# Three single buffers become two or three, and memory attention is handed out in three parts behind the projections

## The chip, the core and the metric

The kernel runs on one core of a Trainium2 chip. The core has five engines that each take their instructions in order: TensorE (PE in the profile), VectorE (DVE), ScalarE (ACT), GpSimd (POOL) and the sync engine (SP), which in this kernel issues every DMA. The metric is device time in microseconds for one execution of the whole program. Before the change it is 2147.47 us, the median of three runs (2147.37 to 2157.03).

## The reference, cut to what matters

One layer over 4096 rows of width 1024. A normalized input is projected once, and three groups of heads read the projection; their gated outputs go through one output projection.

```python
h = _rms(x, norm_gain)
proj = h @ w_in                          # u, v, gate | q, k, v, gate | mem q, mem gate
y_g = _chunked_gmlp(g_u, g_v, ...) * silu(g_gate)      # 4 heads, mixes 128 rows of a chunk
q, k = _rms(a_q, ...), _rms(a_k, ...)                  # 8 heads of 64
y_a = _dilated_attention(q, k, v) * silu(a_gate)       # windows (128,1) (512,4) (2048,16)
qn = _rms(m_q, ...)                                    # 4 heads into 256 memory rows
p = softmax(qn @ mk.T / sqrt(64))
y_m = (p @ mv) * silu(m_gate)
x = x + concat(y_g, y_a, y_m) @ w_out
```

The dilated attention runs the same head at three dilations and weights them by their softmax denominators. The inputs have wide gains, so a true row maximum is taken before each exponential, and every product is made of two halves in 16 bits (a high and a low part) to keep the accuracy.

## The kernel before, in words

The rows are cut into 32 tiles of 128. There are four stretches of the span. Pass A (to about 423 us) normalizes and transposes the rows and projects v and half of q and k. Pass B (`pass_b`, about 423 to 948 us) projects the other half and the attention gate. Pass C (`pass_c`, about 948 to 1774 us) does the gating group and the memory attention, tile by tile; in an iteration n it projects tile n with `wC1` (tile `pc1`), and tile n-2 (`LAG`) with `wC2` and `wC3` (`pc2`, `pc3`). The last stretch merges all and multiplies with `w_out` (`fps`).

The dilated attention runs beside passes B and C as a second stream, `side`, which `merge` advances by so many steps per step of the main one, at a higher priority. For each of the 8 heads it has a part that finds row maxima (`attn_max`) and a main part (`attn_main`); the maxima of head h+1 are found during the main part of head h. In `attn_max`, PE multiplies `qn` and `kp` into `pa` (line 489), DVE takes maxima into `mx` (line 496), these become `mv`, PE transposes them (`pm`, line 513), ACT copies them into a tile of rows `rw` (line 514), a DMA spreads the row out into `cm` (line 515), and DMAs put the result into row 64 of `q2` (line 534), without which the second product of `s` (line 588) can't start. The tiles `qn` and `kp` have one buffer each, so the next head's load (lines 335 to 337) begins after the last `pa` of this head. In `attn_main`, ACT copies the finished outputs from PSUM into `ot` (line 618), from which DMAs store them (lines 623 and 627).

Memory attention of a tile (`mem_attn`) makes a high part `qd` (ACT, line 794) and a low part `q2t` (DVE, line 795), transposes `qd` by a DMA, multiplies it with the memory keys into `mpa` (line 804), takes maxima, puts them into column 64 of `q2t` (line 807), and transposes `q2t` by a DMA into `qm` (line 808); then come scores `ms`, the exponential, `mo`, and `ym`.

The order on each engine is not the order of the code: a scheduler places instructions by their priority (mostly their place in the code, with the offset for the second stream) and by the times that it foresees. A small edit can therefore move rows far away. An engine stands at its next row until that can go, and everything behind waits too; for SP that holds for every DMA of the kernel. Four buffers bear on the change: `rw` has one, of the two dilations 1 and 4 that use it in turn; `ot` has two; `q2t` one for all tiles; and PSUM tiles have two of each tag.

Of the kernel before, what the change touches and what calls it, by code (L numbers as in the profile page):

```python
# [2 lines left out]

# [6 lines left out]
F16 = mybir.dt.float16  # L10
# [8 lines left out]
P = 128  # L19
T = 4096  # L20
D = 1024
NT = T // P
KT = D // P
# [48 lines left out]
def tile_hybrid_layer(ctx, tc, x, mem, norm_gain, w_in, gv_gain, wsT, gb, aqg, akg,  # L72
                      mem_gain, w_kv, mqg, mkg, w_out, out):
    nc = tc.nc
    V, S, G, TE, Q = nc.vector, nc.scalar, nc.gpsimd, nc.tensor, nc.sync
# [6 lines left out]
    def ps_tile(tag, shape, dt, name):  # L82
        return pp.tile(shape, dt, tag="po" if tag == "tr" else tag, name=name)
# [135 lines left out]
    def proj(ps, xt, w, n, c=0):  # L219
        for k in range(KT):  # L220
            for a, b in ((0, 0), (0, 1), (1, 0)):
                TE.matmul(ps[:, :n], xt[:, a, k, :], w[:, b, k, c:c + n],  # L222
                          start=(k == 0 and a == 0 and b == 0), stop=(k == KT - 1 and a == 1))


    def load_rows(pool, src, nm):
# [63 lines left out]
    pm = ctx.enter_context(tc.tile_pool(name="pm", bufs=2))  # L290
# [33 lines left out]
    K1m = cp.tile([P, 4, 256], F16, name="K1m")  # L324
    K2m = cp.tile([65, 4, 256], F16, name="K2m")
# [23 lines left out]
    with tc.tile_pool(name="pA", bufs=2) as pA:  # L349
# [33 lines left out]
        for i in range(2):  # L383
            for n in range(NL):
                if i == 0:
                    vts[n] = pA.tile([P, NH, VW], F16, name=f"vt{n}", tag="vt", bufs=5)
                ps = ps_tile("pj", [P, 512], F32, f"pv{n}_{i}")
# [8 lines left out]
        for n in range(NT):  # L396
# [37 lines left out]
            if n >= NL:  # L434
                ps = ps_tile("pj", [P, 512], F32, f"pv{n}")
# [4 lines left out]
            ps = ps_tile("pj", [P, 512], F32, f"pq{n}")  # L440
# [13 lines left out]
            if n == 12:  # L454
                wM, scM = got("wM")
                for j in range(2):
                    mT = mTs[:, j]
                    ps = ps_tile("pj", [P, 512], F32, f"pm{j}")
# [19 lines left out]
    def attn_max(h, qn, kp):  # L478
        mx = at.tile([P, 96], F32, name=f"mx{h}", tag="mx", bufs=1)
        for ci, d in enumerate(DILS):  # L480
            nb = NT // d
            for u in range(16):
                pa = ps_tile("pa", [P, 2, 256], F32, f"pa{h}_{ci}_{u}")
                for i in range(2):
                    bi = 2 * u + i
                    r, b = bi // nb, bi % nb
                    q0 = r + b * P * d
                    w = 256 if b else 128
                    TE.matmul(pa[:, i, 256 - w:256], qn[:, q0:q0 + (P - 1) * d + 1:d],  # L489
                              packed(kp, d, r, max(b - 1, 0), w), start=True, stop=True)  # L490
                for i in range(2):
                    bi = 2 * u + i
                    w = 256 if bi % nb else 128
                    mc = 64 + (bi % 2) * 16 + bi // 2 if d == 16 else ci * 32 + bi
                    jk = at.tile([P, 256], BF16, name=f"jk{h}_{ci}_{bi}", tag="jk", bufs=1)
                    V.tensor_tensor_reduce(jk[:, :w], pa[:, i, 256 - w:256],  # L496
                                           masks[d][:, 256 - w:256],
                                           1.0, -3e38, ALU.add, ALU.max,
                                           mx[:, mc:mc + 1])
                yield  # L500
        mv = at.tile([P, 96], F16, name=f"mv{h}", tag="mv", bufs=1)
        V.tensor_scalar(mv, mx, -(2.0 ** -15), asg[:, 3:4], ALU.mult, ALU.add)
        cm = at.tile([32, 4, P], F16, name=f"cm{h}", tag="cm", bufs=1)
        Q.dma_start(m_d[h].rearrange("(b p r) -> p b r", b=2, r=16),
                    mv[:, 64:96].rearrange("p (b r) -> p b r", b=2))
        Q.dma_start(cm[:, 2, :], m_d[h].rearrange("(n p) -> n p", p=P))
        for ci, d in enumerate(DILS[0:2]):
            nb = NT // d
            rw = at.tile([nb, P * d], F16, name=f"rw{h}_{ci}", tag="rw", bufs=1)
            pt = ps_tile("tr", [P, 4, P], F16, f"pm{h}_{ci}")  # L510
            for r in range(d):
                c0 = ci * 32 + r * nb
                TE.transpose(pt[:nb, r, :], mv[:, c0:c0 + nb], idh)
            S.copy(rw.rearrange("b (p r) -> b r p", r=d), pt[:nb, :d, :])
            Q.dma_start(cm[:, ci, :], rw.rearrange("b (n p) -> b n p", p=P))
        yield
        V.tensor_tensor(cm[:, 0, :], cm[:, 0, :], cm[:, 1, :], ALU.min)
        ca, cb = (cm[:, i, :].rearrange("n (j r) -> n j r", r=R16) for i in (0, 2))
        V.tensor_tensor(cm[:, 3, :].rearrange("n (r j) -> n j r", r=R16), ca, cb, ALU.min)
        cms[h] = cm  # L520
        yield
# [24 lines left out]
    def attn_main(h, q1, k1):  # L546
# [6 lines left out]
        for ci, d in list(enumerate(DILS))[::ORD]:  # L553
# [20 lines left out]
            for r in range(d):  # L574
                prev = None
                for b0 in range(0, nb, 2):
# [19 lines left out]
                    def pv(r=r, b0=b0, ph=ph, pl=pl, prev=prev, ci=ci, d=d, nb=nb, vblk=vblk, og=og):  # L596
                        for i in range(2):
# [16 lines left out]
                                          start=False, stop=(j == len(terms) - 1))  # L614
                            if slot == 3:
                                ot = at.tile([P, 4, 65], F32, name=f"ot{h}_{ci}_{r}_{b}", tag="ot",
                                             bufs=2)
                                S.copy(ot, o)
                                if d == 4:
                                    ov = o_d[ci].rearrange("(b m r j) h c -> r b m j h c", b=nb,  # L620
                                                           r=d, j=8)
                                    for i in range(4):
                                        Q.dma_start(ov[r, b - 3 + i, :, :, h, :], ot[:, i, :])
                                else:
                                    ov = o_d[ci].rearrange("(x p) h c -> p x h c", p=P)
                                    x1 = r * nb + b + 1
                                    Q.dma_start(ov[:, x1 - 4:x1, h, :], ot)
# [155 lines left out]
    wC1, scC1 = got("wC1")  # L783
    wC3, scC3 = got("wC3")
    fz = cp.tile([P, 4], F32, name="fz")
    q2ts = [pm.tile([P, 4, P], F16, name=f"q2t{i}", bufs=1) for i in range(1)]
    V.memset(q2ts[0], 0.0)

    qms = [None]

    def mem_attn(n, qn):
        qd = pm.tile([P, 4, 2, HD], F16, name=f"qd{n}", tag="hl", bufs=2)
        q2t = q2ts[0]
        S.copy(qd, qn.unsqueeze(2).broadcast_to([P, 4, 2, HD]))
        V.tensor_sub(q2t[:, :, 0:64], qn, qd[:, :, 0, :])
        if n % 2 == 0:
            qms[0] = pm.tile([P, 2, 2, 4, P], F16, name=f"qm{n}", tag="stg", bufs=2)
        Q1m, Q2m = qms[0][:, n % 2, 0], qms[0][:, n % 2, 1]
        Q.dma_start_transpose(Q1m, qd.rearrange("p s a c -> p (s a c)"))
        m4 = pm.tile([P, 4], F32, name=f"m4{n}", tag="m4")  # L800
        for hp in range(2):
            pa = ps_tile("pa", [P, 2, 256], F32, f"mpa{n}_{hp}")
            for i in range(2):
                TE.matmul(pa[:, i, :], Q1m[:, 2 * hp + i, :], K1m[:, 2 * hp + i, :],
                          start=True, stop=True)
            V.tensor_reduce(m4[:, 2 * hp:2 * hp + 2], pa, AX.X, ALU.max)
        V.tensor_scalar(q2t[:, :, 64], m4, -(2.0 ** -15), msg[:, 3:4], ALU.mult, ALU.add)
        Q.dma_start_transpose(Q2m, q2t.rearrange("p s c -> p (s c)"))
        yield
        o = ps_tile("po", [P, 4, 65], F32, f"mo{n}")  # L810
        for hp in range(2):
            st = ps_tile("ps", [P, 2, 2, P], F32, f"ms{n}_{hp}")
            for i in range(2):
                h = 2 * hp + i
                for b in range(2):
                    kk = slice(b * P, (b + 1) * P)
                    TE.matmul(st[:, i, b, :], K1m[:, h, kk], Q1m[:, h, :], start=True,
                              stop=False)
                    TE.matmul(st[:, i, b, :], K2m[:, h, kk], Q2m[0:65, h, :], start=False,
                              stop=True)  # L820
            if not pools:
                e = at.tile([P, 512], F32, name=f"me{n}_{hp}", tag="e", bufs=4)
                ph = at.tile([P, 512], F16, name=f"mph{n}_{hp}", tag="ph", bufs=4)
# [19 lines left out]
        rd = pm.tile([P, 4], F32, name=f"rd{n}", tag="rd")  # L843
        V.reciprocal(rd, o[:, :, 64])
        V.tensor_tensor(ym[n], o[:, :, 0:64], bcast(rd, HD), ALU.mult)
        yield

    ym, vns = {}, {}
    o1 = []
# [12 lines left out]
    def pass_c():  # L862
        xTs = {}
        for n in range(NT + LAG):
# [15 lines left out]
            if n == 1:  # L880
                wC2, scC2 = got("wC2")
                V.tensor_scalar_mul(fz[:, 0:1], scC2[1][:, 2:3], 0.5)
                V.tensor_mul(fz[:, 1:2], fz[:, 0:1], scC2[0][:, 2:3])
                V.tensor_scalar_mul(fz[:, 2:3], scC3[0][:, 2:3], 0.5)
                V.tensor_mul(fz[:, 3:4], fz[:, 2:3], scM[1][:, 0:1])
                V.tensor_scalar_mul(fz[:, 3:4], fz[:, 3:4], 2.0 ** -4)
            if n < NT:
                yield from mem_attn(n, qn)
            if n >= LAG:
                m = n - LAG  # L890
                xT = xTs.pop(m)
# [1 line left out]
                    zp = pm.tile([P, 2, 256], F32, name=f"z{m}", tag="sg", bufs=2)  # L893
                z = zp[:, m % 2]
                ps = ps_tile("pj", [P, 512], F32, f"pc2_{m}")
                proj(ps, xT, wC2, 512)
                S.activation(z, ps[:, 256:512], AF.Tanh, scale=fz[:, 0:1])
                V.scalar_tensor_tensor(z, z, 1.0, ps[:, 256:512], ALU.add, ALU.mult)
                V.scalar_tensor_tensor(z, z, fz[:, 1:2], ps[:, 0:256], ALU.mult, ALU.mult)
                yield  # L900
                ps = ps_tile("pj", [P, 512], F32, f"pc3_{m}")
                pg = ps[:, 256:512].rearrange("p (h c) -> p h c", c=HD)
                vn = vns.pop(m)
                for h in range(4):
                    TE.matmul(pg[:, h, :], wst_g[:, h, :], vn[:, h, :], start=True, stop=True)
                proj(ps, xT, wC3, 256)
                for h in range(4):
                    V.scalar_tensor_tensor(z[:, h * HD:(h + 1) * HD], pg[:, h, :],
                                           gbt[:, h:h + 1], z[:, h * HD:(h + 1) * HD],
# [3 lines left out]
                S.activation(zm, ps[:, 0:256], AF.Tanh, scale=fz[:, 2:3])  # L913
                V.scalar_tensor_tensor(zm, zm, 1.0, ps[:, 0:256], ALU.add, ALU.mult)
                zms[m] = zm
                yield
            if n >= LAG + MLAG:
                mem_gate(n - LAG - MLAG)
# [87 lines left out]
```

## Time and profile before

| what | value |
|---|---|
| median of three runs | 2147.47 us (2147.37 to 2157.03) |
| the profiled execution | 2148.14 us, of which 2146.4 us are the span of its instructions |
| PE busy | 2015.0 us, 94% |
| DVE, ACT, POOL busy | 1457.5, 1199.4, 682.5 us |
| mean granted TensorE clock | 0.976 |

PE is busy for nearly the whole span, so the idle time of another engine counts only where PE ends up standing for it. Such time shows as a wait of PE, and in the granted clock, which falls to half around some of the waits.

### The profile page before, as it was taken

How to read it: one execution, taken by the hardware profiler on the slowest of the kernel's cores; microseconds unless marked ns; L12 is line 12 of the kernel's file. 1: busy time of each engine (PE TensorE's matmuls, PEld its weight loads, DVE VectorE, ACT ScalarE, POOL GpSimd, SP SyncE). 2: the span in 40 equal slices, each digit the busy share in tenths (PEclk: the TensorE clock that was granted, in tenths of full speed). 3: DMA queues.
4: the chain of work that ended last, by engine and by line, in shares of the span. 5: the costliest groups of instructions: out<-in, count | busy, mean ns of one | idle time of the engine just before them, and what ended most of it. 6: DMA issues, size and time to landing. Idle time of an engine off the chain costs nothing.

```text
span 2146.4 us, 45733 instructions
## 1 busy us (share of the span) xinstructions
PE 2015.0 (94%) x17025; PEld 1297.6 (60%) x17025; DVE 1457.5 (68%) x4331; ACT 1199.4 (56%) x2048; POOL 682.5 (32%) x632
## 2 busy tenths in 40 slices
PE   5999999988999899998998998998989999999999
PEld 4444444434466465565775776765766766667766
DVE  7655465466678565687885786776867677777762
ACT  6776565444488476774764675664756753222221
POOL 1212212211155254452553563452635640000000
PEclk8999999999999899999999999999999999999999
DMA  7778677684566768766546357345345357767762
GB/s 220 204 203 198 180 199 168 151 212 138 166 143 174 184 139 193 182 164 157 115 101 156 81 130 182 80 130 117 89 115 122 87 136 213 217 211 220 219 187 69
DMA packets 468959, 341.00 MB, mean 159 GB/s; under 512 B 294400, under 2 KB 404096, under 8 KB 466944
## 3 DMA queue, kind: packets, MB, share of 16 engines
q1 hardware_dynamic: 468736, 338.08, 61.4%
q8 instruction: 133, 2.18, 0.4%
q14 instruction: 90, 0.74, 0.1%
HBM read 198.52 MB, written 113.84 MB: 146 GB/s over the span
## 4 chain that ended last, share of the span: by engine, by line
PE 40%; DMA 9%; DVE 7%; ACT 3%; issue 2%; SPq 1%; POOL 1%; ACTq 0%; DVEq 0%; POOLq 0%
PE fps L222 14%; PE pc L222 11%; PE s L586 2%; PE s L588 2%; PE pa L489 2%; DMA od<-ot 1%; DMA qm<-q2t 1%; DVE e L591 1%; DMA cm<-rw 1%; PE fpt L771 1%; DVE jk L496 1%; PE pqb L222 1%; PE pag L222 1%; DMA fo<-od 1%; PE o L613 1%
## 5 line engine op out<-in xcount | busy, mean ns | idle before, releaser
L543 POOL TENSOR_TENSOR pl<-e,ph 128x512 f16<-128x512 f32 (+1 forms) x384 | 409.3, 1079 | 350.2 <-ACT ph L542 267.4
L222 PE MATMUL pc<-wC,xTc 128*128 128x512 f16 (+1 forms) x2304 | 477.1, 350 | 9.5 <-DMA xTc<-xTd 3.3
L496 DVE CUSTOM_DVE_ANT_0 jk<-pa,mask 128x256 bf16<-128x256 f32 (+1 forms) x768 | 299.4, 390 | 92.0 <-PE pa L489 72.8
L222 PE MATMUL fps<-wO,fyT 128*128 128x256 f16 (+1 forms) x2304 | 341.2, 309 | 0.0
L593 ACT ACTIVATE e<-e,gas 128x512 f32<-128x512 f32 (+1 forms) x384 | 252.3, 673 | 124.8 <-DVE e L591 122.7
L222 PEld LDWEIGHTS <-xTc 128*128 128x128 f16 x2304 | 222.9, 100 | 161.0 <-issue 11.8
L222 PEld LDWEIGHTS <-fyT 128*128 128x128 f16 x2304 | 224.4, 98 | 102.2 <-issue 2.3
L591 DVE TENSOR_TENSOR e<-s,mask 128x512 f32<-128x512 f32 (+1 forms) x384 | 233.4, 626 | 66.6 <-PE s L588 59.3
L222 PEld LDWEIGHTS <-xTa 128*128 128x128 f16 x1608 | 158.3, 100 | 176.7 <-issue 12.1
L222 PEld LDWEIGHTS <-xTb 128*128 128x128 f16 x1536 | 149.4, 99 | 154.3 <-issue 14.0
L269 POOL TENSOR_TENSOR r_q<-r_q,mhalf 128x8 f32<-128x8 f32 x64 | 114.4, 1789 | 371.3 <-DVE r_q L267 357.8
L542 ACT CAST ph<-e 128x512 f16<-128x512 f32 (+1 forms) x384 | 211.0, 568 | 26.7 <-PE o L613 19.9
L222 PE MATMUL pqb<-wQ,xTb 128*128 128x512 f16 x768 | 188.0, 385 | 1.8 <-DVE sc_wC L179 1.8
L222 PE MATMUL pag<-wAG,xTb 128*128 128x512 f16 x768 | 186.1, 383 | 2.2 <-ACT rw_q L257 2.1
L586 PE MATMUL s<-q,k 128*128 128x256 f16 (+1 forms) x768 | 178.8, 265 | 9.6 <-DVE e L591 4.1
L222 PE MATMUL pv<-wV,xTa 128*128 128x512 f16 (+1 forms) x840 | 179.4, 370 | 5.8 <-DVE vt L285 5.2
L609 PE MATMUL o<-vr,ph 128*128 128x65 f16 x1368 | 172.0, 194 | 9.9 <-ACT ph L542 6.6
L222 PE MATMUL pq<-wQ,xTa 128*128 128x512 f16 x768 | 173.6, 381 | 1.1 <-DVE wQ L174 0.7
L588 PE MATMUL s<-q,k 65*128 65x256 f16 (+1 forms) x768 | 170.7, 265 | 4.1 <-DMA q<-cm 4.0
L611 PE MATMUL o<-vr,ph 128*128 128x64 f16 x1368 | 170.3, 194 | 0.0
L489 PE MATMUL pa<-kp,qn 128*128 128x256 f16 (+1 forms) x768 | 136.2, 269 | 36.3 <-DVE mx L496 15.6
L613 PE MATMUL o<-vr,pl 128*128 128x65 f16 x1368 | 160.4, 193 | 5.5 <-POOL pl L543 5.1
(282 smaller groups left out, 3364.6 us busy)
## 6 DMA issues: line engine op xcount, KB each, us to landing
vr<-vd SPq DMA_DIRECT2D x48, 520.0 KB
fo<-od SPq DMA_DIRECT2D x96, 260.0 KB
od<-ot SPq DMA_DIRECT2D x128, 130.0 KB
x_a<-in_x_dram SPq DMA_DIRECT2D x32, 512.0 KB
xTd<-xTa SPq DMA_DIRECT2D x32, 512.0 KB
xTb<-xTd SPq DMA_DIRECT2D x32, 512.0 KB
xTc<-xTd SPq DMA_DIRECT2D x32, 512.0 KB
fx<-in_x_dram SPq DMA_DIRECT2D x32, 512.0 KB
```

Of the source, the lines that this page charges most:

```text
L222: TE.matmul(ps[:, :n], xt[:, a, k, :], w[:, b, k, c:c + n], start=(k == 0 and a == 0 and b == 0), stop=(k == KT - 1 and a == 1))
L489: TE.matmul(pa[:, i, 256 - w:256], qn[:, q0:q0 + (P - 1) * d + 1:d], packed(kp, d, r, max(b - 1, 0), w), start=True, stop=True)
L496: V.tensor_tensor_reduce(jk[:, :w], pa[:, i, 256 - w:256], masks[d][:, 256 - w:256], 1.0, -3e38, ALU.add, ALU.max, mx[:, mc:mc + 1])
L542: S.copy(ph[:, :w], e[:, :w])
L543: G.tensor_sub(pl[:, :w], e[:, :w], ph[:, :w])
L586: TE.matmul(st[:, i, :n], k1[:, kk], packed(q1, d, r, b, n), start=True, stop=False)
L588: TE.matmul(st[:, i, :n], k2[:, kk], packed(q2, d, r, b, n), start=False, stop=True)
L591: V.tensor_tensor(e[:, :w], st.rearrange("p a q -> p (a q)")[:, :w], masks[d][:, :w], ALU.add)
L593: S.activation(e[:, :w], e[:, :w], AF.Exp, scale=asg[:, 2:3])
L609: TE.matmul(o[:, slot, 0:65], hi[:, c:c + 128], v[:, 0:65], start=(j == 0), stop=False)
L611: TE.matmul(o[:, slot, 0:64], hi[:, c:c + 128], v[:, 66:130], start=False, stop=False)
L613: TE.matmul(o[:, slot, 0:65], lo[:, c:c + 128], v[:, 0:65], start=False, stop=(j == len(terms) - 1))
```

## The change

`rw` gets a tag for each of the two dilations, and so two buffers; `ot` gets three; `q2t` two, used by tiles in turn (the second one is cleared at the start, one more DVE instruction). `mem_attn` becomes a generator in three parts that `pass_c` advances by hand. The first part (high and low part of the query, and the transpose of the high part) is issued as before. The second (the maxima, `mpa`) is handed the last matmul of the `wC2` projection of the same iteration and its matmuls get an edge that places them behind it on PE; it is written after that projection now, and was written ahead of it. The third (`ms` and on) is handed the last matmul of the `wC3` projection and is written after that; it too was ahead of both. The edges set an order on one engine and no semaphore.

```diff
     def proj(ps, xt, w, n, c=0):
...
-                TE.matmul(ps[:, :n], xt[:, a, k, :], w[:, b, k, c:c + n],
+                last = TE.matmul(ps[:, :n], xt[:, a, k, :], w[:, b, k, c:c + n],
...
+        return last.ins
...
-            rw = at.tile([nb, P * d], F16, name=f"rw{h}_{ci}", tag="rw", bufs=1)
+            rw = at.tile([nb, P * d], F16, name=f"rw{h}_{ci}", tag=f"rw{ci}", bufs=1)
...
-                                             bufs=2)
+                                             bufs=3)
                                 S.copy(ot, o)
...
-    q2ts = [pm.tile([P, 4, P], F16, name=f"q2t{i}", bufs=1) for i in range(1)]
-    V.memset(q2ts[0], 0.0)
+    q2ts = [pm.tile([P, 4, P], F16, name=f"q2t{i}", bufs=1) for i in range(2)]
+    for q2t in q2ts:
+        V.memset(q2t, 0.0)
...
     def mem_attn(n, qn):
-        q2t = q2ts[0]
+        q2t = q2ts[n % 2]
...
         Q.dma_start_transpose(Q1m, qd.rearrange("p s a c -> p (s a c)"))
+        ins = yield
         m4 = pm.tile([P, 4], F32, name=f"m4{n}", tag="m4")
...
+            with after(ins):
+                for i in range(2):
+                    TE.matmul(pa[:, i, :], Q1m[:, 2 * hp + i, :], K1m[:, 2 * hp + i, :],
...
         Q.dma_start_transpose(Q2m, q2t.rearrange("p s c -> p (s c)"))
-        yield
+        ins = yield
...
+                    with after(ins):
+                        TE.matmul(st[:, i, b, :], K1m[:, h, kk], Q1m[:, h, :], start=True,
...
+    def after(ins):
+        return nullcontext() if ins is None else tc.issue_after(ins)
...
             if n < NT:
-                yield from mem_attn(n, qn)
+                ma = mem_attn(n, qn)
+                next(ma)
             if n >= LAG:
...
-                proj(ps, xT, wC2, 512)
+                ins = proj(ps, xT, wC2, 512)
...
                 yield
+            if n < NT:
+                ma.send(ins)
+                yield
+            if n >= LAG:
                 ps = ps_tile("pj", [P, 512], F32, f"pc3_{m}")
...
-                proj(ps, xT, wC3, 256)
+                ins = proj(ps, xT, wC3, 256)
...
                 zms[m] = zm
+                yield
+            if n < NT:
+                for _ in (0,):
+                    try:
+                        ma.send(ins)
```

What the scheduler makes of it shows at three places. The first is ACT at the end of head 5's maxima, where `rw5_0` and `rw5_1` are the two rows of that head and `ag_wO00` is a scale of the output weights, which PE's projections queue behind. Before:

```order
L618 COPY ot4_0_0_27_17559<-o4_0_0_24_17502 128x260
L514 COPY rw5_0_17520<-pm5_0_17521 32x128
L514 COPY rw5_1_17525<-pm5_1_17526 8x4x128
L169 COPY ag_wO00_18520<-pt_wO00_18513 128x8
L172 ACTIVATE wO0_18512<-st_wO00_18004,ag_wO00_18520 128x256 x2
L618 COPY ot4_0_0_31_17641<-o4_0_0_28_17616 128x260
```

And now:

```order
L544 CAST ph4_0_0_30_17545<-e4_0_0_30_17542 128x384
L516 COPY rw5_0_17522<-pm5_0_17523 32x128
L516 COPY rw5_1_17527<-pm5_1_17528 8x4x128
L620 COPY ot4_0_0_31_17643<-o4_0_0_28_17618 128x260
L927 ACTIVATE zm11_18320<-pc3_11_18286,fz_11985 128x256
L169 COPY ag_wO00_18522<-pt_wO00_18515 128x8
```

The two `rw` copies stand side by side in both, but the second has a buffer of its own now; the same rows of ACT queue behind it.

The second place is SP, a little later, where the loads of the next head's keys and queries (`kp_6`, `qn_6`) and those of head 5's main part (`q1_5`, `q2`, `k2`) are issued. Before, the second half of `qn_6` stands 18 rows behind the first half, which is out of these rows:

```order
L506 DMA cm5_17517<-md5_113 32x128
L346 DMA q1_5_17562<-qkpd1_103 64x1024
L347 DMA q1_5_17562<-qkpd1_103 64x1024
L532 DMA q2_4312<-qkpd1_103 64x1024
L515 DMA cm5_17517<-rw5_1_17525 32x1x128
L533 DMA k2_4313<-knd1_99 64x1024
L627 DMA od0_105<-ot4_0_0_31_17641 128x4x65
L337 DMA qn_6_17861<-qnd1_101 64x4096
L534 DMA q2_4312<-cm5_17517 1x8x128 x4
```

And now:

```order
L868 DMA yd10_158<-zm10_17817 128x256
L337 DMA kp_6_17843<-qkpd1_103 128x4096
L338 DMA qn_6_17842<-qnd1_101 64x4096
L339 DMA qn_6_17842<-qnd1_101 64x4096
L506 DMA md5_113<-mv5_17517 128x2x16
```

The load of head 6 is issued in one piece, and PE's first `pa` of head 6 is placed earlier with it.

The third place is DVE in pass C, where the low part of tile 13's query is made. Before, it stands behind the work of tile 14:

```order
L873 TENSOR_TENSOR rw_c14_18576<-rw_c14_18576,r_c14_18580 128x256
L875 TENSOR_TENSOR vn14_18589<-rw_c14_18576,r_c14_18580 128x256
L899 SCALAR_TENSOR_TENSOR z12_18875<-z12_18875,fz_11985,pc2_12_18876 128x256
L795 TENSOR_TENSOR q2t0_11986<-rw_c13_18037,qd13_18114 128x4x64
L496 ISA jk6_0_0_17870,mx6_17866<-pa6_0_0_17867,mask1_830 128x128
```

And now:

```order
L881 TENSOR_TENSOR rw_c13_18039<-rw_c13_18039,r_c13_18043 128x256
L883 TENSOR_TENSOR vn13_18052<-rw_c13_18039,r_c13_18043 128x256
L884 TENSOR_TENSOR vn13_18052<-vn13_18052,gvg_839 128x256
L798 TENSOR_TENSOR q2t1_11987<-rw_c13_18039,qd13_18116 128x4x64
L908 SCALAR_TENSOR_TENSOR z10_17685<-z10_17685,pc2_11_18120 128x256
```

It follows its own tile's work directly now, since it does not wait for tile 12's transpose to have read the only buffer.

## Rows read from the trace of the kernel before

**Rows 1.** The page: span, and busy time with its share and instructions.
```profile
span 2146.4 us, 45733 instructions
...
PE 2015.0 (94%) x17025; PEld 1297.6 (60%) x17025; DVE 1457.5 (68%) x4331; ACT 1199.4 (56%) x2048; POOL 682.5 (32%) x632
```

**Rows 2.** Stretches: length, then PE, PEld, DVE, ACT, POOL busy, clock, DMA share, GB/s.
```profile
423.00:948.00 525.00, 483.38 (x3808) 283.97 (x3806) 364.39 (x1243) 332.48 (x583) 196.56 (x164) 0.97 0.68 170
948.00:1774.00 826.00, 776.56 (x8174) 557.39 (x8172) 610.32 (x1918) 502.60 (x979) 394.64 (x349) 0.97 0.50 122
```

**Rows 3.** Waits of PE, 423 to 1774 us: total, times, longest.
```profile
PE pa L489 <- DMA qn<-qnd: 10.6, 2, 7.4
PE pa L489 <- issue: 8.1, 3, 4.1
...
PE s L588 <- DMA q<-cm: 4.0, 2, 3.1
PE s L586 <- DMA q<-qkpd: 3.3, 1, 3.3
...
PE pc L222 <- DVE sc_wO L179: 2.7, 1, 2.7
PE pc L222 <- DVE zm L914: 2.6, 1, 2.6
PE ms L817 <- DVE e L591: 2.5, 1, 2.5
```

**Rows 4.** Waits of ACT, same stretch.
```profile
ACT rw L514 <- DMA cm<-rw: 39.5, 8, 10.7
...
ACT ot L618 <- DMA od<-ot: 22.2, 11, 6.4
```

**Rows 5.** Waits of DVE, same stretch.
```profile
DVE q2t L795 <- DMA qm<-q2t: 32.9, 22, 3.9
```

**Rows 6.** Waits of SP, same stretch.
```profile
SPq L627 <- ACT ot L618: 156.6, 66, 8.0
```

**Rows 7.** Timeline of ACT at head 5's rows: start, duration, instruction, idle before it.
```profile
1293.25 1.28 ACT L514 COPY rw<-pm 8x512 f16<-8x512 f16 x1 [7.76 <-DMA cm<-rw]
```

**Rows 8.** Timeline of DVE, shortly after.
```profile
1307.55 0.42 DVE L795 TENSOR_TENSOR q2t<-rw_c,qd 128x256 f16<-128x256 f32 x1 [3.26 <-DMA qm<-q2t]
```

**Rows 9.** Timeline of PE, two single waits.
```profile
1000.84 0.33 PE L489 MATMUL pa<-kp,qn 128*128 128x128 f16 x2 [3.52 <-issue]
...
1454.78 0.19 PE L609 MATMUL o<-vr,ph 128*128 128x65 f16 x1 [1.66 <-ACT ot L618]
```

**Rows 10.** Short stretches around waits of PE, columns as in rows 2.
```profile
698.00:712.00 14.00, 7.34 (x22) 2.97 (x23) 4.02 (x17) 2.00 (x4) 0.00 (x0) 0.51 1.10 298
865.00:869.00 4.00, 4.00 (x18) 1.99 (x17) 1.49 (x5) 3.32 (x4) 0.00 (x0) 0.57 1.00 246
1002.00:1005.00 3.00, 3.00 (x8) 1.06 (x7) 1.54 (x6) 0.62 (x1) 0.00 (x0) 0.50 0.74 201
1142.00:1145.00 3.00, 3.00 (x33) 2.54 (x32) 0.14 (x2) 0.89 (x2) 0.80 (x1) 0.50 0.36 82
1295.00:1299.00 4.00, 4.00 (x11) 1.44 (x12) 2.64 (x8) 3.97 (x11) 0.00 (x0) 0.57 0.69 162
1309.00:1316.00 7.00, 6.63 (x65) 5.69 (x65) 6.56 (x19) 6.09 (x13) 4.15 (x5) 0.51 1.05 335
1456.00:1466.00 10.00, 6.66 (x37) 5.13 (x36) 3.32 (x13) 2.71 (x4) 0.00 (x0) 0.50 0.60 120
1606.00:1609.00 3.00, 3.00 (x9) 1.09 (x8) 2.60 (x8) 2.15 (x6) 0.00 (x0) 0.50 0.63 70
```

**Rows 11.** The chain that ended last, in the last stretch: start, us, what.
```profile
1832.25 10.42 PE fps L222 x72
```

**Rows 12.** Timeline of the start, DVE and ACT.
```profile
2.88 0.27 DVE L787 MEMSET q2t<- 128x256 uint32 x1
...
9.69 1.06 ACT L236 ACTIVATE xj_a<-x_a 128x1024 bf16<-128x1024 f32 x1 [0.21 <-DMA x_a<-in_x_dram]
```

More of the change, by code (lines that the diff above doesn't have):

```diff
@@ L1 @@
 import math
-from contextlib import ExitStack
+from contextlib import ExitStack, nullcontext
 import concourse.bass as bass
@@ L221, in proj @@
             for a, b in ((0, 0), (0, 1), (1, 0)):
-                TE.matmul(ps[:, :n], xt[:, a, k, :], w[:, b, k, c:c + n],
-                          start=(k == 0 and a == 0 and b == 0), stop=(k == KT - 1 and a == 1))
+                last = TE.matmul(ps[:, :n], xt[:, a, k, :], w[:, b, k, c:c + n],
+                                 start=(k == 0 and a == 0 and b == 0),
+                                 stop=(k == KT - 1 and a == 1))
+        return last.ins
     def load_rows(pool, src, nm):
@@ L802, in mem_attn @@
             pa = ps_tile("pa", [P, 2, 256], F32, f"mpa{n}_{hp}")
-            for i in range(2):
-                TE.matmul(pa[:, i, :], Q1m[:, 2 * hp + i, :], K1m[:, 2 * hp + i, :],
-                          start=True, stop=True)
+            with after(ins):
+                for i in range(2):
+                    TE.matmul(pa[:, i, :], Q1m[:, 2 * hp + i, :], K1m[:, 2 * hp + i, :],
+                              start=True, stop=True)
             V.tensor_reduce(m4[:, 2 * hp:2 * hp + 2], pa, AX.X, ALU.max)
@@ L816, in mem_attn @@
                     kk = slice(b * P, (b + 1) * P)
[L817 to L820, printed above, removed]
+                    with after(ins):
+                        TE.matmul(st[:, i, b, :], K1m[:, h, kk], Q1m[:, h, :], start=True,
+                                  stop=False)
+                        TE.matmul(st[:, i, b, :], K2m[:, h, kk], Q2m[0:65, h, :], start=False,
+                                  stop=True)
             if not pools:
@@ L845, in mem_attn @@
         V.tensor_tensor(ym[n], o[:, :, 0:64], bcast(rd, HD), ALU.mult)
-        yield
+    def after(ins):
+        return nullcontext() if ins is None else tc.issue_after(ins)
     ym, vns = {}, {}
@@ L886, in pass_c @@
                 V.tensor_scalar_mul(fz[:, 3:4], fz[:, 3:4], 2.0 ** -4)
+            ma, ins = iter(()), None
             if n < NT:
-                yield from mem_attn(n, qn)
+                ma = mem_attn(n, qn)
+                next(ma)
             if n >= LAG:
@@ L915, in pass_c @@
                 zms[m] = zm
+                yield
[3 more added lines that the diff above has]
+                        ma.send(ins)
+                    except StopIteration:
+                        pass
                 yield
```

## The prediction, made before the changed kernel was run

> **What bounds the kernel now.** I read the page first, then the stretches, then the waits of each engine, and last the timeline around single waits. The page shows PE busy for 94% of the span, the next engine for 68% [rows 1]. So time comes off only where PE stands or runs slowly. In passes B and C, where all edits but the clear at the start act, PE stands for 525.0 - 483.4 + 826.0 - 776.6 = 91.0 us, and its mean clock is 0.97 [rows 2]. That is all that the change can reach.
>
> The reader is to see the distance between an engine's wait and PE's. ACT stands 39.5 us in eight spells until a DMA has read `rw`, and 22.2 us in eleven until a store has read `ot` [rows 4]; DVE stands 32.9 us in 22 spells for `q2t` [rows 5]. These are the three buffers, 94.6 us together, but other engines work meanwhile. What of it reaches PE I take from its own waits [rows 3] and from who was behind the stalled row.
>
> The clock adds to this. Around several waits of PE it is granted at half (1.2 of 2.4 GHz): 0.57 over 4 us behind the wait at 861, 0.50 over 3 us at 1142, 0.51 over 14 us at 698, of which PE is busy 7.34 [rows 10]. Busy time times the missing share of the clock is what a stretch loses: 7.34 x 0.49 = 3.6 us in the first, 4.00 x 0.43 = 1.7 in the second.
>
> **The change part by part.**
>
> *Two `rw` buffers.* ACT's eight spells go. The order shows what stands behind the second `rw` copy of head 5: `ag_wO`, from which DVE makes `sc_wO`. In the trace ACT stood 7.76 us there [rows 7], and PE then waited 2.7 us for `sc_wO`. At head 7's rows the same happens with `zm`, 2.6 us. And the second half of `cm` goes out sooner, which the first `q<-cm` loads await; PE stood 4.0 us for these in two waits [rows 3]. These loads also stand behind other rows of SP and behind the maxima of dilation 16, so I count half, 2.0. Waits: 2.7 + 2.6 + 2.0 = 7.3. Clock: 1.7 at 1295, 1.5 at 1606, and half of the 1.7 at 865 [rows 10], 4.0. Together 11.3, between 0 (PE's rows, placed anew, wait for something else) and 9.3 + 4.9 = 14.2.
>
> *The third `ot` buffer.* One spell reached PE plainly: ACT stood 6.4 us (the longest of rows 4), PE 1.66 for the copy [rows 9], and then 3.3 for `q<-qkpd` [rows 3], a load whose row on SP stands behind the store of that `ot`. That is 5.0, and 6.66 x 0.50 = 3.3 of clock at 1456 [rows 10].
>
> *Two `q2t` buffers.* DVE stood 3.26 us with the softmax rows of the dilated attention behind it [rows 8], so that `e` came late for `ms`: 2.5 us on PE [rows 3], and 6.63 x 0.49 = 3.2 of clock at 1309 [rows 10]. The other 21 spells end under other PE work.
>
> For `ot` and `q2t` together that is 7.5 of waits and 6.5 of clock, 14.0. A buffer more moves such a wait on only if the store or transpose that it waited for gets away. Here SP is the question: it stood 156.6 us in 66 spells at these very stores, waiting for ACT's copy [rows 6], and a row that can't go holds all DMAs behind it. The Trainium skill says in "DMA: Bandwidth & Descriptors", section "Where the ~2 µs actually goes", that a semaphore wait of a DMA happens on the issuing sequencer before dispatch, not in the DMA engines. The trace agrees with its 66 spells. By that rule alone the wait would only pass from ACT to SP and the 14.0 would be 0; by the rows a part was ACT's own. I take half, 7.0, between 0 and 14.0.
>
> *The order at the heads' ends.* `qn` and `kp` stay single, so the next head's first `pa` can't start before they are loaded. What covers this is the PE work placed between. A column costs 10.42 us / 24,576 = 0.424 ns (72 matmuls, 24 of 512 and 48 of 256 columns) [rows 11]. Counting the columns between the last `pa` of a head and the first of the next in the order gives covers, from head 0 to head 6, of 9.4, 6.8, 10.6, 11.2, 9.8, 15.0, 11.1 us before, and 9.4, 11.6, 8.5, 11.6, 8.9, 9.1, 10.1 now. (The 15.0 are 48 matmuls of 512 columns, 17 of 256, 8 of 128 and 84 small ones, 35,319 columns; now 19, 27, 16 and 43, 21,466.) PE waited 3.2 and 7.4 for `qn` at the first two, 3.5 at the fourth [rows 3, 9], 4.1 at the fifth and 0.5 at the seventh: the load needs about 12.6, 14.2, 14.7, 13.9 and 11.6, and at most 10.6 at the third, where nothing was waited for. With 13.9, and the middle between that and what they themselves showed for the third and the last, the waits now are 3.2, 2.3, 3.7, 3.1, 5.0, 4.8 and 2.6, sum 24.7 against 18.7. Clock: 3.6 + 1.5 + 1.5 = 6.6 before, and 1.5 for each of four waits over 3 us that moved, 6.0. So this costs 6.0 - 0.6 = 5.4.
>
> *The edges of memory attention.* In the order before, `mpa` of each of the 30 tiles from 2 on already stands behind the last `pc2` matmul of its iteration, and `ms` behind the last `pc3`; they bind nowhere there. What changes is their place in the code, and so priority. `ym` is wanted three iterations later, and an iteration is 826/32 = 26 us [rows 2]. I take 0. From both sides: the 2.5 us that `ms` waits could come once more, or go (they are counted above).
>
> *The start.* DVE has a second clear, 0.27 us, before it waits for the loaded weights, and on ACT the square of the second row tile (`xj_a`, 1.06 us) is placed ahead of the copy of the first tile's transpose, which so also waits for that load at 9.69 [rows 12]. PE works off the first projections until the next weights land, and these set its next start. I take 0; at most the 1.06 and the 0.27 come out at the end, 1.3.
>
> Sum on the profiled execution: 2148.1 (span 2146.4 [rows 1] and 1.7 around it) - 11.3 - 7.0 + 5.4 = 2135.2. That execution was 0.7 above the median of the runs shown, 2147.5, so the forecast is 2134.5, in round 2134.
>
> **The rivals.**
>
> *No change: the waits come back on SP.* The 66 spells of rows 6 speak for it, and that PE's rows are placed anew in both passes, so each removed wait meets another neighbour. Against it is that `sc_wO` and `zm` hang on ACT's copy alone. Then only these two return, with their clock: 2.7 + 2.6 + 1.7 + 1.5 = 8.5, less the 5.4 at the heads: 2147.5 - 3.1 = 2144. The rule of the Trainium skill stands on this side.
>
> *Slower: PE stands at every head's first `pa`.* The place is the seven ends of heads, the mechanism the shorter cover for a load that has not become shorter. If it needs 14.7 each time but the first, the waits are 3.2, 3.1, 6.2, 3.1, 5.8, 5.6 and 4.6, 31.6 or 12.9 more; and if those over 4.5 each cost the 3.6 of the stretch at 698, the clock loses 4 x 3.6 + 2 x 1.5 = 17.4, or 10.8 more. The buffers return half of 18.3 then: 2147.5 + 23.7 - 9.2 = 2162. It decides from the point where these waits take more than about 29 us over the 25.3 of now (to be slower by half a percent with 18.3 returned), or 20 with half of it. For it speak the five covers below 11 us, against it that the third and seventh ends needed no more than 10.6 and 11.6.
>
> *All of it returns.* 14.2 + 14.0, and the heads' ends as before: 2147.5 - 28.2 = 2119. I keep it as the lower end of the forecast.
>
> **How the numbers follow.** Half a percent, 10.7 us, is about what a measurement of this kernel can tell from no change; faster means below 2136.8. Forecast 55% (2119 to 2141), no change 33%, slower 12%. Of the forecast about 7 points lie above 2136.8, of the second case 5 below it; of the third 2 lie within half a percent. That gives 0.53 faster, 0.37 the same, 0.10 slower. The range goes from the end at which all returns, 2118, to 2152, between the second case and the third; about a tenth is left out on each side at most. The likeliest case's own range is 2119 to 2141.
>
> **What would show it.** Right: ACT's wait of `rw` for `cm<-rw` is gone, `ot`'s falls from 22.2 to less than half, DVE's for `q2t` likewise; PE's waits for `sc_wO`, `zm` and `q<-cm` are small, and its idle time in passes B and C falls from 91 to about 80, with a higher clock there. The waits for `qn` and those called issue at `pa` sum to about 25 instead of 18.7, with the wait at head 1's end down from 7.4 and a new one at head 5's. The last stretch, from the first regular `fps`, is as long as before. Wrong: SP's wait for `ot` grows by what ACT's fell, with PE's idle time unchanged (the second case); or the `pa` waits go over 40 us (the third).

## The result, and the profile after

The changed kernel took 2124.95 us (median of 4 runs, 2118.87 to 2129.16), the kernel before beside it 2149.51 us (4 runs, 2147.37 to 2157.03). The ratio is 0.9873, with a 95% interval of 0.9854 to 0.9891, so 1.3% faster. The forecast was 2134, the range 2118 to 2152. The execution that was profiled took 2122.38 us.

The page after, its first lines:

```profile
span 2120.7 us, 45749 instructions
...
PE 1999.8 (94%) x17025; PEld 1291.9 (61%) x17025; DVE 1467.6 (69%) x4332; ACT 1204.4 (57%) x2048; POOL 685.2 (32%) x632
```

Against [rows 1] the span is 25.7 us shorter. PE's busy time fell by 15.2 with the same 17025 matmuls, and its idle time (span less busy) from 131.4 to 120.9, by 10.5. Part of the smaller busy time is the granted clock, whose mean over the span went from 0.976 to 0.982. By the trace's record of the granted clock, PE's busy time in the stretches at half speed, times the missing half, is 39.7 us before and 29.9 after, 9.8 less. The other 5.4 us of busy time are not explained: without the clock's loss it is 1975.3 us before and 1969.9 after, and over the profiles of all fourteen kernels it goes from 1968 to 1976.

The stretches of pass B, of pass C and of the tail from the first regular `fps` (after, columns as in [rows 2]):

```profile
423.00:948.00 525.00, 487.96 (x3873) 287.94 (x3870) 375.93 (x1273) 338.03 (x590) 201.49 (x168) 0.97 0.69 171
948.00:1749.00 801.00, 758.68 (x8136) 549.93 (x8133) 613.08 (x1902) 503.80 (x975) 392.22 (x345) 0.99 0.53 127
1749.00:2120.70 371.70, 362.86 (x2796) 252.55 (x2794) 233.12 (x563) 94.52 (x95) 2.31 (x2) 0.99 0.63 187
```

Pass B is as long as it was. Pass C is 25 us shorter, and there the clock rose from 0.97 to 0.99. PE stands 37.0 + 42.3 = 79.3 us in the two, 11.7 less than [rows 2]. The tail runs from 1749.0 to the end, 371.7 us, against 2146.4 - 1774 = 372.4.

What PE waited for in passes B and C (after; total, times, longest, as in [rows 3]):

```profile
PE pa L491 <- DVE mx L498: 16.5, 13, 3.6
PE pa L491 <- DMA qn<-qnd: 15.4, 6, 4.6
PE o L615 <- POOL pl L545: 8.0, 16, 0.8
PE ms L825 <- DMA qm<-q2t: 6.2, 3, 3.1
PE s L588 <- DMA q<-qkpd: 4.6, 1, 4.6
PE mpa L809 <- DMA qm<-qd: 4.1, 4, 1.7
...
PE s L590 <- DMA q<-cm: 2.6, 2, 1.8
...
PE ms L823 <- DVE e L593: 0.9, 1, 0.9
```

`sc_wO` and `zm`, 2.7 and 2.6 before, are in no row any more, and neither is a wait of `o` for the copy of `ot`. The waits for `qn` and those called issue at `pa`, 18.7 before, are 15.4 now, where the forecast had 24.7. The largest row, `pa` for the maxima of DVE, hardly moved (15.6 before). Two rows of memory attention grew: `mpa` had none for its transposed query, and `ms` had this (before):

```profile
PE ms L819 <- DMA qm<-q2t: 2.2, 3, 1.0
```

ACT, DVE and SP in the same stretch (answers to [rows 4], [rows 5] and [rows 6]):

```profile
ACT rw L516 <- PE pm L515: 8.6, 7, 2.4
...
ACT ot L620 <- DMA od<-ot: 0.3, 1, 0.3
```

```profile
DVE cm L519 <- DMA cm<-rw: 18.2, 6, 5.2
...
DVE q2t L798 <- DMA qm<-q2t: 17.4, 8, 5.0
```

```profile
SPq L629 <- ACT ot L620: 156.5, 67, 7.5
...
SPq L625 <- ACT ot L620: 23.6, 13, 4.1
```

ACT's eight spells for `rw` against the DMA are gone, and `ot`'s all but one of 0.3 us. DVE's for `q2t` fell from 22 to 8, and their time from 32.9 to 17.4 us, a little over half. SP's wait for `ot` at the store of line 629 is what it was, 156.6 before. At the other store, line 625, it grew by 5.0 us; before:

```profile
SPq L623 <- ACT ot L618: 18.6, 17, 2.6
```

The copy that [rows 7] showed behind 7.76 us of waiting, and its neighbours on ACT now:

```profile
1267.04 0.26 ACT L516 COPY rw<-pm 32x128 f16<-32x128 f16 x1 [0.73 <-PE pm L515]
1269.35 1.30 ACT L516 COPY rw<-pm 8x512 f16<-8x512 f16 x1 [2.05 <-PE pm L515]
```

It waits 2.05 us, and for PE's own transpose. Two single waits of PE after, the one at head 1's end, and the longest that is new:

```profile
706.94 0.91 PE L491 MATMUL pa<-kp,qn 128*128 128x128 f16 x4 [3.58 <-DMA qn<-qnd]
...
1275.25 0.42 PE L588 MATMUL s<-q,k 128*128 128x256 f16 x2 [4.58 <-DMA q<-qkpd]
```

At 706.94 it stands 3.58 us where it was 7.4 [rows 3]. The stretches of pass C with the clock at half (after, columns as in [rows 10]):

```profile
1006.00:1009.00 3.00, 2.75 (x21) 2.35 (x21) 0.92 (x4) 1.27 (x2) 0.00 (x0) 0.51 0.60 130
1276.00:1279.00 3.00, 3.00 (x8) 1.06 (x7) 1.95 (x8) 0.00 (x0) 0.00 (x0) 0.50 0.73 157
1300.00:1303.00 3.00, 3.00 (x23) 2.50 (x22) 2.68 (x14) 3.00 (x7) 0.92 (x1) 0.50 0.38 97
1573.00:1576.00 3.00, 3.00 (x16) 2.07 (x15) 1.23 (x4) 0.00 (x0) 0.00 (x0) 0.50 1.20 327
1737.00:1740.00 3.00, 3.00 (x9) 1.08 (x8) 1.49 (x7) 0.07 (x1) 0.00 (x0) 0.51 0.84 243
```

There are five, 17 us together by the trace's record of the granted clock; before there were nine with 44. By that record (busy time times the missing share) pass C lost 20.3 us before and 8.4 after: 11.9 of its gain. The clock fell behind a wait in both: at 1276 it is half behind the 4.58 above.

### The profile page after: what moved, and what is told of

Read it like the earlier page. It is cut to its first block, busy times and chain, and to the rows that moved or that the text cites. A ratio compares the mean times of both kernels' runs of the same rounds, so it can differ in the third digit from the quotient of the medians.

```text
span 2120.7 us, 45749 instructions
## 1 busy us (share of the span) xinstructions
PE 1999.8 (94%) x17025; PEld 1291.9 (61%) x17025; DVE 1467.6 (69%) x4332; ACT 1204.4 (57%) x2048; POOL 685.2 (32%) x632
## 4 chain that ended last, share of the span: by engine, by line
PE 52%; DMA 6%; DVE 6%; issue 3%; ACT 3%; SPq 1%; POOL 1%; ACTq 0%; DVEq 0%; POOLq 0%
PE fps L222 15%; PE pc L222 13%; PE pag L222 4%; PE pqb L222 3%; PE s L588 3%; PE s L590 3%; PE pa L491 2%; PE o L615 1%; PE o L613 1%; PE o L611 1%; PE fpt L773 1%; DMA qn<-qnd 1%; DVE e L593 1%; DVE jk L498 1%; DMA qm<-q2t 1%
```

## The experiments

The question is whether the gain belongs to the buffers one by one, as the sum had it, to the parts, or to a chance order, since the order of PE's instructions differs in nearly every version. An order is no time, but it says what a run can tell. Without the edges the changed kernel gives the same program, every instruction in the same place. So the edges bind nothing, as forecast; what the three parts do, they do by their place in the code.

Each ratio is against executions of the kernel before beside it. Their median was 2149.5 us beside the changed kernel, and 2156.5, 2161.6 and 2152.1 in the three later sessions (first four experiments, next four, last four). So ratios can be put side by side, but not the times of different sessions.

**One buffer at a time, and an order by itself.** First `ot` alone, which hardly touches the order (16 rows of PE):

```diff
-                                             bufs=2)
+                                             bufs=3)
```

> The kernel before with three ot buffers and nothing else. The order of all engines stays as before but for 16 rows of PE, 6 of ACT, 4 of SP and 2 of DVE, so this is the buffer without a new order. Theory of buffers: ACT's 22.2 us of waits for the stores fall to under 8, and the wait of PE at head 6 goes with its clock, 4 to 8 us in all: 2140 to 2146. Theory of order (the gain is in where the scheduler put the rows): no change within 3 us.

Ratio 0.9988 [0.9966, 1.0011] (the 95% interval in brackets, here and below). ACT's waits in passes B and C:

```profile
ACT rw L514 <- DMA cm<-rw: 42.9, 7, 11.2
...
ACT rw_c L257 <- DVE q2t L795: 17.9, 7, 5.8
```

No row has `ot` waiting for its store, 22.2 us before [rows 4], and the time is the same. In this order the 22.2 were worth nothing that can be measured.

Then a second `q2t` that is cleared and never used, so that no wait can go for a buffer, and the order changes (14793 of PE's 33519 rows stand elsewhere):

```diff
-    q2ts = [... for i in range(1)]
-    V.memset(q2ts[0], 0.0)
+    q2ts = [... for i in range(2)]
+    for q2t in q2ts:
+        V.memset(q2t, 0.0)
```

> The kernel before with a second q2t buffer that is cleared at the start and never used. No wait can go for a buffer, but the scheduler places 14793 of 33519 rows of PE otherwise. Theory of buffers: within 4 us of before. Theory of order: it moves by 5 to 20 us, to either side.

Ratio 0.991 [0.9876, 0.9944]. ACT and DVE wait for the single buffers no less than before:

```profile
ACT rw L514 <- DMA cm<-rw: 45.3, 7, 10.8
...
ACT ot L618 <- DMA od<-ot: 24.2, 13, 3.3
```

```profile
DVE q2t L796 <- DMA qm<-q2t: 50.3, 20, 8.2
```

An instruction of 0.27 us [rows 12] at the start, and a buffer that nothing reads, gave 0.9%, with longer waits on DVE than in [rows 5]. So no ratio of another order within about a percent may be put down to a buffer without more.

`rw` alone:

```diff
-            rw = at.tile([nb, P * d], F16, name=f"rw{h}_{ci}", tag="rw", bufs=1)
+            rw = at.tile([nb, P * d], F16, name=f"rw{h}_{ci}", tag=f"rw{ci}", bufs=1)
```

> The kernel before with two rw buffers and nothing else; the order changes from head 0's rows on. Theory of buffers: 10 to 14 us faster, ACT's 39.5 us for cm<-rw gone, PE's waits for sc_wO, zm and q<-cm small. Theory of order: any of -20 to +10, not tied to those waits.

Ratio 1.0021 [1.0006, 1.0035]. ACT, then DVE:

```profile
ACT rw_c L257 <- DVE q2t L795: 23.3, 6, 8.1
ACT ot L618 <- DMA od<-ot: 17.9, 13, 3.7
```

```profile
DVE q2t L795 <- DMA qm<-q2t: 40.7, 23, 4.5
...
DVE cm L517 <- DMA cm<-rw: 20.7, 7, 5.4
```

The 39.5 us went as forecast, and the time did not fall. DVE waits 40.7 for `q2t` instead of 32.9, and 20.7 for `cm`. In `rw_c L257` ACT itself waits 23.3 us behind that `q2t` (the copy of the next projection waits until DVE has read the earlier one). Before, this was:

```profile
ACT rw_c L257 <- DVE q2t L795: 18.1, 6, 5.8
```


`q2t` alone, used in turn:

```diff
+    q2ts = [... for i in range(2)]
...
+        q2t = q2ts[n % 2]
```

> The kernel before with two q2t buffers used in turn and nothing else. Theory of buffers: 3 to 6 us faster, DVE's 32.9 us for q2t down to under 18. Theory of order: about what the kernel with the unused second buffer does, since the same clear is added, or any other shift of 5 to 20 us.

Ratio 0.994 [0.9921, 0.9959]. Its order is not the placebo's, so it is no proof of a buffer either. ACT, then DVE:

```profile
ACT rw L514 <- DMA cm<-rw: 35.7, 6, 10.4
...
ACT ot L618 <- DMA od<-ot: 24.8, 13, 5.1
```

```profile
DVE q2t L796 <- DMA qm<-q2t: 20.3, 11, 3.8
```

DVE's wait for `q2t` fell from 32.9 to 20.3, the `rw_c` wait behind it is gone, and the waits for `rw` and `ot` stayed.

**The parts, and all buffers.** The three parts with the buffers of before:

```diff
-                yield from mem_attn(n, qn)
+                ma = mem_attn(n, qn)
+                next(ma)
```

> The memory attention issued in three parts, with the buffers of before (one rw, two ot, one q2t). Theory of buffers: no change within 5 us, the edges bind nowhere. Theory of order: the later place of mpa and ms in the code is what gave the new order of pass C, so most of the gain is here, 15 to 25 us faster, in pass C (825 us before, 802 with all).

Ratio 1.0003 [0.9981, 1.0024]. DVE:

```profile
DVE q2t L797 <- DMA qm<-q2t: 44.6, 21, 7.1
```

The parts by themselves bring nothing, where 15 to 25 us had been expected if the order decides. The three buffers without the parts (the diffs above together):

> The three buffers, with memory attention issued as before. Theory of buffers: nearly the whole gain, 20 to 27 us faster. Theory of order: anything between the unused second buffer's 0.991 and two rw buffers' 1.002, so 0 to 20 us faster, with pass C at 815 us or more.

Ratio 0.9919 [0.9896, 0.9941]. `rw` waits for PE alone, `ot` 0.4 us for its store, and DVE:

```profile
DVE q2t L796 <- DMA qm<-q2t: 24.0, 10, 5.2
```

This is some of the gain, and by its interval not all: the parts add to the buffers, by 0.9919 against 0.9873, or the other order does.

**One piece taken out of the changed kernel.** `ot` back to two buffers, in nearly the same order (two rows of ACT differ):

```diff
-                                             bufs=3)
+                                             bufs=2)
```

> The changed kernel with two ot buffers instead of three. The order is that of the changed kernel but for 2 rows of ACT, so this is the third ot buffer by itself in the new order. Theory of buffers: 5 to 8 us of the gain go, ratio to before 0.990 or more. Theory of order: as the changed kernel, 0.985 to 0.989.

Ratio 0.9915 [0.9893, 0.9937], against 0.9873 with three: the third `ot` buffer is worth 0.4% here, some 9 us, and with the two intervals taken together 0.1 to 0.7%. ACT:

```profile
ACT ot L620 <- DMA od<-ot: 22.5, 16, 3.5
```

The same 22 us of waiting on ACT, 22.2 in [rows 4], measured 0.1% (-0.1 to 0.3) in the order of before and 0.4% beside two `rw` and two `q2t`. That is the one pair of comparisons in which the order hardly moves on either side. The intervals overlap, so the pair suggests that the worth of this buffer depends on the other two, and does not show it.

Each `q2t` cleared twice, to give the changed kernel another order (5363 of PE's 33530 rows):

```diff
     for q2t in q2ts:
         V.memset(q2t, 0.0)
+        V.memset(q2t, 0.0)
```

> The changed kernel with each q2t cleared twice at the start, two DVE instructions of 0.27 us more, which lets the scheduler place 5363 of 33530 rows of PE otherwise; all buffers and parts as in the changed kernel. Theory of buffers: as the changed kernel, 0.985 to 0.989 of before. Theory of order: moves from it by 3 to 15 us, most likely slower.

Ratio 0.985 [0.9818, 0.9882]: the gain does not hang on that exact order. But of the other orders this is the nearest: counted in the traces by operation, tile and shape, 3447 of PE's 17025 matmuls stand at another place, against 6456 to 9765 in the versions with one `q2t`, without the parts, or with one `rw`. No version was faster by more than the intervals tell.

`rw` and `ot` together, in the kernel before:

> The kernel before with two rw and three ot buffers. Each of them alone gave 1.002 and 0.999 of before. If the two waits stand in one row on ACT at the heads' ends, so that each alone only lets the other be waited for, the two together give 0.990 to 0.995; if they are worth what they are worth alone, 1.001 or so; if the order decides, 0.990 to 1.004 with ACT's two waits gone and nothing to show for it.

Ratio 0.9983 [0.9958, 1.0009]. DVE:

```profile
DVE q2t L795 <- DMA qm<-q2t: 39.8, 19, 5.5
DVE cm L517 <- DMA cm<-rw: 24.7, 7, 4.9
```

Both waits of ACT are gone (`ot` 1.5), and the single `q2t` is waited for longer than before. Then the changed kernel with one `rw`:

```diff
-            rw = at.tile([nb, P * d], F16, name=f"rw{h}_{ci}", tag=f"rw{ci}", bufs=1)
+            rw = at.tile([nb, P * d], F16, name=f"rw{h}_{ci}", tag="rw", bufs=1)
```

> The changed kernel with one rw buffer. The forecast's largest term was this buffer, 11.3 us: a ratio of 0.992 or 0.993 to before if it is worth that, 0.985 to 0.989 if it is worth nothing in this company, 0.995 or more if the three buffers only work together.

Ratio 1.0028 [1.0008, 1.0048]. ACT, then DVE:

```profile
ACT rw L516 <- DMA cm<-rw: 38.2, 7, 10.6
...
ACT rw_c L259 <- DVE q2t L798: 6.7, 2, 4.1
```

```profile
DVE q2t L798 <- DMA qm<-q2t: 36.2, 16, 4.1
```

With one `rw`, the two `q2t` are waited for as long as the one was before: 36.2 against 17.4 in the changed kernel. Last, the changed kernel with one `q2t`:

```diff
-        q2t = q2ts[n % 2]
+        q2t = q2ts[0]
```

> The changed kernel with one q2t buffer. The forecast gave this buffer less than 3 us: 0.986 to 0.990. If the three parts of memory attention need a free q2t to gain anything (with the buffers of before they gave 1.000), the part of the gain that came with them goes too: 0.992 or more.

Ratio 1.0001 [0.9984, 1.0018]. DVE, then ACT:

```profile
DVE q2t L797 <- DMA qm<-q2t: 49.0, 23, 9.7
```

```profile
ACT rw_c L259 <- DVE q2t L797: 25.6, 8, 7.5
```

Without the second `q2t`, ACT stands 25.6 us behind it, in place of the waits for `rw`.

**How far an order alone goes.** The kernel before with its `q2t` cleared four times:

```diff
-    V.memset(q2ts[0], 0.0)
+    for _ in range(4):
+        V.memset(q2ts[0], 0.0)
```

> The kernel before with q2t cleared four times at the start, three DVE instructions of 0.27 us more; no buffer and no part of the change. The scheduler places 16992 of 33516 rows of PE otherwise than before, and 9865 otherwise than with the unused second buffer, which gave 0.991. If the order before was an unlucky draw, this is faster too, 0.988 to 0.996; if draws scatter round it, as likely slower as faster, 0.993 to 1.007; if the order hardly matters, 0.998 to 1.002.

Ratio 1.0032 [1.0011, 1.0054]. The two orders that differ by clears alone lie at -0.9% and +0.3%, and the parts with the buffers of before, which change the order alone too, at 0.0%.

**All of them side by side.** "Buffer waits" is my own sum over passes B and C (423 to 1774 us) of four rows of each profile: ACT's `rw` for `cm<-rw`, ACT's `ot` for `od<-ot`, DVE's `q2t` for `qm<-q2t`, and ACT's `rw_c` behind DVE's `q2t`. For the kernel before it is 39.5 + 22.2 + 32.9 + 18.1 = 112.7.

| kernel | buffer waits, us | ratio [95%] |
|---|---|---|
| changed | 17.7 | 0.9873 [0.9854, 0.9891] |
| changed, cleared twice | 23.2 | 0.985 [0.9818, 0.9882] |
| three buffers | 24.4 | 0.9919 [0.9896, 0.9941] |
| changed, two `ot` | 39.3 | 0.9915 [0.9893, 0.9937] |
| `rw` + `ot` | 56.9 | 0.9983 [0.9958, 1.0009] |
| changed, one `q2t` | 74.9 | 1.0001 [0.9984, 1.0018] |
| `q2t` | 80.8 | 0.994 [0.9921, 0.9959] |
| `rw` | 81.9 | 1.0021 [1.0006, 1.0035] |
| changed, one `rw` | 83.1 | 1.0028 [1.0008, 1.0048] |
| `ot` | 90.2 | 0.9988 [0.9966, 1.0011] |
| parts | 99.5 | 1.0003 [0.9981, 1.0024] |
| before | 112.7 | 1 |
| before, cleared four times | 120.6 | 1.0032 [1.0011, 1.0054] |
| before, cleared and unused | 135.3 | 0.991 [0.9876, 0.9944] |

The sum was formed after the runs. Read with that care, it says: from 135 down to 57 us the ratio does not follow it, and lies between 0.991 and 1.003; the four kernels with two `rw` and two `q2t`, below 40 us, lie between 0.985 and 0.992. No single buffer, added alone, accounts for the 1.3%.

PE's own idle time in the same stretch, 91.1 us before, follows the time more closely. In the one profile of each kernel it is 79.4 us in the changed kernel and 79.3 in the one cleared twice, the two fastest, and 88 to 106 in the other eleven. The four kernels of one session (cleared twice, two `ot`, three buffers, parts) have 79.3, 90.7, 91.7 and 98.4, in the order of their ratios. The three buffers alone have 91.7 with buffer waits of 24.4, and the one cleared twice 79.3 with 23.2. So the buffer waits are no measure of the gain: what of them reaches PE differs from kernel to kernel.

## Why the prediction was right, and where its steps were not

**The time and its direction were right, the case too.** The measured 2124.95 lies in the likeliest case's own range (2119 to 2141), 5 us under its middle. On the profiled execution the sum gave 2135.2, and it took 2122.38, 12.8 less. That it came so near is in part luck: its largest term measured nothing by itself, and an order, which no term prices, moved the time by up to 0.9%, or 19 us.

**PE's idle time.** The sum's terms took 7.3 and 7.5 / 2 of waits off and put 6.0 back at the heads' ends, 5.1 in all; the signs said "from 91 to about 80". It is 79.3. The signs had the better number, but the two were not the same, and the terms were too small by 6.6. The clock below adds 1.7 to the miss, and PE's busy time in the two passes fell by 3.7 more than the clock explains, for which there was no term; the tail gave 0.7.

**The clock.** The terms' net was 4.0 + 3.25 + 0.6 = 7.9. By the trace's record passes B and C lost 29.2 us before and 19.6 after, 9.6 less: 11.9 in pass C, while B lost 2.3 more. The stretches behind `q<-cm` (865), `sc_wO` (1295) and `ot` (1456) of [rows 10] have no successor. The one behind `e` for `ms` (1309), 3.2 us of loss, became the one at 1300: PE is busy 3.00 us in it, at 0.50, so it loses 1.5.

**The heads' ends: the step with the wrong sign.** I let the `qn` load need 13.9 us at the later heads and had waits of 24.7, 6.0 more than before. They came to 15.4, 3.3 less. At the third to the seventh end PE waited 4.62, 1.61, 1.45, 0 and 0.78 over covers of 8.5, 11.6, 8.9, 9.1 and 10.1, so the load needed 13.1, 13.2, 10.4, at most 9.1, and 10.9. At the fifth and sixth that is 3.5 and at least 4.8 us less than the 13.9 taken from an end of before. The load itself is the same, so its need is not carried over from one order to another. (The waits are in the fence below; the first two ends waited 3.38 and 3.58 over covers of 9.4 and 11.6, no less need than before.)

```profile
843.21 0.50 PE L491 MATMUL pa<-kp,qn 128*128 128x128 f16 x2 [4.62 <-DMA qn<-qnd]
...
996.29 0.33 PE L491 MATMUL pa<-kp,qn 128*128 128x128 f16 x2 [1.61 <-DMA qn<-qnd]
...
1136.35 0.54 PE L491 MATMUL pa<-kp,qn 128*128 128x128 f16 x4 [1.45 <-DMA qn<-qnd]
...
1415.04 0.54 PE L491 MATMUL pa<-kp,qn 128*128 128x128 f16 x4 [0.78 <-DMA qn<-qnd]
```

The trace says where the time went. From the issue of the second half of `qn` to the first `pa` it took 12.7 and 13.8 us at the fourth and fifth ends before, and 11.1 and 10.0 now. At the seventh this is 9.8 and 10.2, but SP issued the load 3.4 us behind the last `pa` before and 0.9 now. Why the load was quicker at the fourth and fifth is not shown. The new wait that the signs had at head 5's end, the sixth, did not come. One reading was wrong too: at the third end before, the need was taken as at most 10.6 because nothing was waited for, but the cover holds only columns, and with PE's other waits 13.5 us passed there between the last `pa` (836.30) and the next head's first (850.13). The need of 13.1 now fits that. The heads' ends are the largest mis-sized term: 6.0 - (-3.3) = 9.3 us, of which other waits took 2.7 back.

**Waits that the sum did not have.** PE's waits for the two transposes of memory attention (`ms` and `mpa` for `qm`) went from 2.2 to 10.3 us, where the part on the edges took 0. They are not the parts' doing alone: with the three buffers and no parts they are 15.1. And the 3.3 us for `q<-qkpd`, counted with `ot`, did not go: one such wait is 4.6 now, at another head.

**The wait for `rw`.** That it would go was right; that it alone is worth 11.3 was not borne out: `rw` alone measured 1.0021. The bound "0, PE's rows, placed anew, wait for something else" is what happened there, and the runs of `rw` alone and of `rw` and `ot` point at the single `q2t`: DVE waited 40.7 and 39.8 for it instead of 32.9, and ACT behind it 23.3 and 15.6 against 18.1, so that this part grew in one of them only. That PE's time went there is not shown. Taking `rw` out of the changed kernel costs 1.0028 / 0.9873 = 1.6%, and one `q2t` 1.0001 / 0.9873 = 1.3%. The sum treated the three buffers as independent terms. The runs agree with waits that stand in for one another, which is argued and not shown, since the order moves with each buffer: with `rw` single, the doubled `q2t` is still waited for 36.2 us, and with `q2t` single, ACT stands 25.6 behind it although `rw` is double.

**The waits did not come back on SP.** That was the rival at 33%. If it were so, ACT's 22.2 us for `ot` would have come up at SP. SP's waits for the copy of `ot` are 156.5 + 23.6 against 156.6 + 18.6, 4.9 more, and ACT's went to 0.3. The Trainium skill ("DMA: Bandwidth & Descriptors", section "Where the ~2 µs actually goes") says that a DMA's semaphore wait is served by the issuing sequencer, which is where it stands; it does not say that a wait taken from ACT becomes one of SP. That step was the prediction's own. Nor did PE stand at each head's end, the rival that was slower.

**The edges and the start** were taken as 0. The edges change no row; the parts' place in the code does. The start cannot be told apart: the second clear costs 0.27 us itself, and places about half of PE's rows anew, with -0.9% and +0.3% in two kernels that have only that. I had bounded it at 1.3 us, which was wrong as a bound: I counted the instruction and not the order that it sets off.

**What stays open.** How much of the 1.3% is joint effect of the buffers and how much the luck of the order. The versions with one piece less differ from the changed kernel at 6456 (`q2t`) and 9765 (`rw`) of PE's 17025 matmuls, so each of these ratios holds an order as well as a buffer. What an order does was seen in three draws of the kernel before only, up to 0.9%; where tiles lie in memory changes with a buffer too and was not varied by itself. The four kernels with both buffers, in three orders of PE, are the four at 0.992 or below, but for one at 0.991 without them. That speaks for the buffers; it doesn't split the gain. More buffers (a fourth `ot`, a third `q2t`, a second `qn` or `kp`) have no room in on-chip memory beside these, and were not tried.

## What to carry to other kernels

Where a program places instructions from a list, first measure kernels in which the order alone is moved; a gain smaller than their spread can't be put down to the edit. Buffers whose waits may stand in for one another are to be tried together too and then taken out one at a time: here `rw` and `ot`, tried alone, showed nothing. A wait of an engine that isn't the bound is worth what PE's own waits and its clock behind them give back, and that changes with what else is still waited for.

## What the runs showed of the hardware

Four executions of the same changed program had spans of 2117.2, 2120.7, 2125.8 and 2127.4 us at mean granted clocks of 0.984, 0.982, 0.980 and 0.978: the longer the span, the lower the clock, and 0.006 x 2000 us of PE's busy time is 12 us, about the 10.2 between the ends. The kernel before follows this more loosely: of its 31 executions in the last session, one had a span of 2147.5 us at 0.974 and one of 2152.7 at 0.977. So the clock goes with a part of the scatter, and which of the two comes first is not shown. In the change itself the clock gave 9.8 of the 25.7 us by the trace's record.
